# The second MLP matrix by a seven-product block scheme over pairs of token tiles

## The chip, the cores and the metric

One core of a Trainium2 chip runs the whole program. The metric is the device time of one execution in microseconds. Engines: PE (matmul), PEld (its weight loads), DVE (VectorE), ACT (ScalarE), POOL (GpSimd), SP (SyncE, which here only issues transfers).

## The reference

One layer of a hybrid backbone on 128 context and 1024 latent tokens of width 1024: two mixers, then the MLP, which the change is about. All in float32:

```
h = RMSNorm_pre2(x) * (1 + scale2) + shift2
f = square(relu(h @ W1))          # W1: 1024 x 4096
f = f @ W2                        # W2: 4096 x 1024
x = x + gate2 * RMSNorm_post2(f)
```

## The kernel before

There are NT = 1152 tokens in nine tiles of 128. A float32 product is done as three matmuls: each operand is split into a rounded high part (an ACT copy to a reduced form) and a low part (a DVE subtraction), and high·high, high·low and low·high are added in PSUM.

**First matrix.** The 32 hidden blocks of 128 go in pairs p; pairs 0 and 1 plainly (`plain`), pairs 2 to 15 by a block scheme (`strassen`): the operand matrices are cut in two by two blocks, seven products of sums replace eight, and four more steps do the last 384 tokens. A pair is 11 steps of 12 matmuls 128x384. Hooks by step number put the weight sums and splits of the next pair between the steps. `store` (L2087) squares the result and sends it to DRAM (`Fd`).

**Second matrix.** 16 groups g of two hidden blocks each. `g_load` (L2182) reads back the features and two 128x1024 tiles of W2, `g_w` (L2190) and `g_f` (L2197) split them. `mlp2` (L2236) does nine token tiles with two halves of 512 columns each: six matmuls (L2245 to L2247) into one PSUM bank, and a *take*, in which DVE adds the bank to an accumulator in SBUF (L2251), or in group 0 ACT copies it (L2249). The loads and splits for the next group are hooks behind tiles 1, 2, 4 and 6. In the last group `finish_a` and `finish_b` (L2217, L2222) normalize a tile, multiply it with its gate (L2228), add x (L2230, on POOL but for the last tile) and write it out.

Every engine does its row in the order in which the program was written; a tile framework adds semaphores for data, for the reuse of a buffer, and for a pool laid over the room of a closed one. SP issues all transfers of this part, in order: an issue whose data isn't ready holds those behind it.

## Time and profile before

| what | us |
|---|---|
| median of 3 runs | 1738.44 (1736.56 to 1738.83) |
| profiled execution | 1739.05 |
| its span | 1737.3 |
| last pair (p = 15) | 1298.8 to 1321.73 |
| second matrix and output | 1321.73 to 1737.3 |

Busy shares of the span: PE 93%, DVE 64%, ACT 40%, POOL 17%. These are means over stages with different limits, so they don't tell what the second matrix waits for; that is read from its own stretch. 1.75 us of the execution lie outside the span.

### The profile page before, as it was taken

What the parts mean: (1) busy time and instruction counts of PE and PEld (TensorE: products, weight loads), DVE (VectorE), ACT (ScalarE), POOL (GpSimd) and SP (SyncE); (2) the same over time, 40 slices, a digit from 0 to 9 for tenths busy, and PEclk for the clock granted to TensorE, in tenths of its full rate; (3) what the DMA queues carried; (4) which work ended last, traced back from release to release, by engine and by line L of the source; (5) the groups of instructions that cost most, each with busy time, mean ns of one, the idle gap of its engine ahead of it and who ended that gap; (6) DMA issues with size and microseconds to landing.
All of it is one profiled execution on the core that took longest, in us unless ns stands there. A gap on an engine that the chain in (4) does not pass through costs nothing.

```text
span 1737.3 us, 32874 instructions
## 1 busy us (share of the span) xinstructions
...
## 2 busy tenths in 40 slices
...
GB/s 312 189 138 131 208 138 192 160 190 124 148 152 110 162 177 166 198 227 244 199 181 90 123 105 118 121 112 107 94 89 209 77 93 120 115 82 91 140 49 145
DMA packets 317464, 253.09 MB, mean 146 GB/s; under 512 B 102776, under 2 KB 286272, under 8 KB 315264
## 3 DMA queue, kind: packets, MB, share of 16 engines
...
## 4 chain that ended last, share of the span: by engine, by line
PE 70%; DVE 13%; DMA 6%; POOL 5%; issue 2%; ACT 2%; SPq 2%; DVEq 0%; POOLq 0%; ACTq 0%
PE ps_g L2151 7%; PE ps_P L2151 7%; PE ps_g L531 4%; PE ps_G L2151 3%; PE ps_g L532 3%; PE ps_g L533 3%; PE ps_g L1662 3%; POOL ar L1028 2%; POOL ar L1024 2%; PE ps_m L2247 2%; PE ps_g L2247 2%; PE ps_m L2246 2%; PE ps_g L2246 2%; PE ps_m L2245 2%; PE ps_g L2245 2%
## 5 line engine op out<-in xcount | busy, mean ns | idle before, releaser
L531 PE MATMUL ps_g<-hH,wH 128*128 128x384 f32 x552 | 208.5, 378 | 1.8 <-DVE hH L270 1.2
L532 PE MATMUL ps_g<-hL,wH 128*128 128x384 f32 x552 | 191.2, 346 | 5.6 <-DVE hL L484 5.3
L533 PE MATMUL ps_g<-hH,wL 128*128 128x384 f32 x552 | 189.8, 344 | 0.0
L2230 POOL TENSOR_TENSOR rT1H<-rA,rT1H 128x512 f32<-128x512 f32 x2 | 2.9, 1444 | 804.0 <-DVE rA L2228 804.0
L2193 ACT ACTIVATE ws<-w2r 128x1024 fp32r<-128x1024 f32 x32 | 32.4, 1054 | 272.3 <-DVE rA L2251 126.7
L2151 PE MATMUL ps_P<-h2H,ws 128*128 128x384 f32 x448 | 122.7, 334 | 0.0
L531 PEld LDWEIGHTS ps_g<-hH,wH 128*128 128x128 f32 x552 | 107.1, 194 | 17.3 <-issue 8.4
L532 PEld LDWEIGHTS ps_g<-hL,wH 128*128 128x128 f32 x552 | 107.3, 194 | 10.5 <-DVE hL L484 9.3
L533 PEld LDWEIGHTS ps_g<-hH,wL 128*128 128x128 f32 x552 | 107.0, 194 | 0.0
L1028 POOL TENSOR_TENSOR ar<-ar 128x252 f32<-128x252 f32 (+22 forms) x124 | 89.0, 718 | 9.2
L1024 POOL TENSOR_TENSOR ar<-ar 128x252 f32<-128x252 f32 (+22 forms) x124 | 81.1, 654 | 41.6 <-DMA ar<-NAd 32.1
L2151 PEld LDWEIGHTS ps_P<-h2H,ws 128*128 128x128 f32 x448 | 81.7, 188 | 0.0
L2151 PE MATMUL ps_P<-h2L,ws 128*128 128x384 f32 x224 | 74.9, 334 | 0.0
L1539 DVE TENSOR_TENSOR SV<-ps_m,Dt 64x256 f32<-64x256 f32 x136 | 57.0, 421 | 22.7 <-PE ps_m L1534 19.6
L2132 DVE TENSOR_TENSOR ws<-w1r,ws 128x512 fp32r<-128x512 f32 x56 | 37.2, 687 | 53.0 <-ACT ws L2131 53.0
L2251 DVE TENSOR_TENSOR rA<-ps_G,rA 128x512 f32<-128x512 f32 x68 | 46.8, 688 | 36.6 <-PE ps_G L2247 36.6
L1503 PE MATMUL ps_G<-SV,r 128*32 128x64 f32 x1152 | 54.8, 230 | 13.1 <-DVE SV L1539 12.7
L2251 DVE TENSOR_TENSOR rA<-ps_m,rA 128x512 f32<-128x512 f32 x67 | 46.2, 689 | 28.4 <-PE ps_m L2247 28.4
L2251 DVE TENSOR_TENSOR rA<-ps_g,rA 128x512 f32<-128x512 f32 x67 | 46.1, 689 | 27.2 <-PE ps_g L2247 27.0
L1503 PEld LDWEIGHTS ps_G<-SV,r 128*32 128x32 f32 x1152 | 40.7, 114 | 28.1 <-DVE SV L1539 20.4
L1534 PEld LDWEIGHTS ps_m<-SV,IT 128*64 128x64 f32 x1120 | 42.0, 143 | 25.9 <-issue 10.6
L2151 PE MATMUL ps_g<-h2H,ws 128*128 128x384 f32 x224 | 59.3, 335 | 0.0
...
## 6 DMA issues: line engine op xcount, KB each, us to landing
...
```

The costliest lines, as they stand in the source:

```text
L531: T.matmul(ps, wH[:, k, :], hH[b][:, k, :], start=(k == 0), stop=False)
L532: T.matmul(ps, wH[:, k, :], hL[b][:, k, :], start=False, stop=False)
L533: T.matmul(ps, wL[:, k, :], hH[b][:, k, :], start=False, stop=(k == 7))
L1024: E.tensor_tensor(out=t, in0=X[:, :, 0:m, j:j + 1].to_broadcast([128, 2, m, w]), in1=n[:, :, j % 8:j % 8 + 1, j + 1:32].to_broadcast([128, ...
L1028: E.tensor_tensor(out=X[:, :, 0:m, j + 1:32], in0=X[:, :, 0:m, j + 1:32], in1=t, op=ALU.subtract)
L1503: T.matmul(RU[n][r0:r0 + 32, 0, p, :], KRG[n][kq][:, e, p, kc, 0:32], SV[n][s % NSV][:, e, p, :], start=True, stop=True)
L1539: Q.add("V", cv(256), lambda e=e, ks=ks: V.tensor_tensor(out=SV[n][(s + 1) % NSV][ks, e], in0=x["S"][ks], in1=dv[ks], op=ALU.mult), r=[("S ...
L2151: T.matmul(ps[ch], w[:, qw, k], h[q][:, k, :], start=(new and k == n == 0), stop=(k == 3 and n == 2), skip_group_check=True)
L2245: T.matmul(ps, tok(fH, m), wH[:, hs_], start=(m == 0), stop=False)
L2246: T.matmul(ps, tok(fH, m), wL[:, hs_], start=False, stop=False)
L2247: T.matmul(ps, tok(fL, m), wH[:, hs_], start=False, stop=(m == 1))
L2251: V.tensor_tensor(out=acc_(i)[:, hs_], in0=ps, in1=acc_(i)[:, hs_], op=ALU.add)
```

## The change

The second matrix goes by the same kind of scheme. Eight groups have four hidden blocks each (two pairs, e = 0 and 1). Token tile 8 (context) is done plainly, 24 matmuls; tiles (0,3), (1,4), (2,5), (6,7) are pairs u, each done in seven steps s (`STEP2`) of six matmuls 128x512 on sums of feature blocks and of weight blocks, each step with one take. The four x steps add into one PSUM bank, which is taken after each of them.

The sums S1 to S4 of the features are made behind each pair of the first stage (`f_sums`: three POOL adds, one DVE) and stored beside the features; a pair's features now stand in one set of tiles (`ft`) instead of six rotating buffers. The weight sums T1 to T4 are made on POOL (`w_t`); weights and sums are split by `w_s`, high part on ACT, low part on POOL but where `V` is given. Features come back in 128-token tiles (`f_load`) and are split by `f_h` (ACT) and `f_l` (DVE, three pieces); `c_split` does the context tile. In the last pair, STEPZ reorders the steps, and hooks do group 0's loads and splits. The pool `ac` with the accumulators is laid over the closed pool `dp`, in which `ft` and `fS` lie. The finishing is spread over the last group.

```diff
+    Fd = [dr.tile([128, 7, 512], F32, name=f"Fd{p}") for p in range(NP)]
+    Fc = [dr.tile([128, 2, 128], F32, name=f"Fc{p}") for p in range(NP)]
+    pD, pDp = ExitStack(), ExitStack()
...
-    dp = pool_(pD, "dp", 1)
+    wsp = pool_(pD, "wsp", 1)
+    dp = pool_(pDp, "dp", 1)
...
+        put(m // 2, m % 2)
+        if m % 2:
+            f_sums(m // 2)
...
+        if not ft:
+            ft[0], ft[1] = [dp.tile([128, 3, 512], F32, name=f"ft{i}") for i in range(2)]
+            ft["S"] = dp.tile([128, 4, 512], F32, name="fS")
+        if b < 2:
+            f = ft[i][:, b, 0:BLK]
+        else:
+            f, src = ft[i][:, :, BLK:512], src.rearrange("p (a c) -> p a c", a=3)
...
+    def put(p, i, bs=(0, 1)):
+        for b in bs:
+            if (i, b) != (0, 1):
+                SY.dma_start(out=Fd[p][:, i + (b if i else 0)], in_=ft[i][:, b])
+        SY.dma_start(out=Fc[p][:, i], in_=ft[i][:, 2, BLK:512])
+    def f_sums(p):
+        t = ft["S"]
+        (a11, a21), (a12, a22) = [[ft[i][:, b] for b in range(2)] for i in range(2)]
+        G.tensor_tensor(out=t[:, 0], in0=a21, in1=a22, op=ALU.add)
+        V.tensor_tensor(out=t[:, 2], in0=a11, in1=a21, op=ALU.subtract)
+        G.tensor_tensor(out=t[:, 1], in0=t[:, 0], in1=a11, op=ALU.subtract)
+        G.tensor_tensor(out=t[:, 3], in0=a12, in1=t[:, 1], op=ALU.subtract)
+        SY.dma_start(out=Fd[p][:, 3:7], in_=t)
...
+    STEPZ = tuple(STEPS[i] for i in (0, 1, 2, 3, 7, 4, 5, 6, 9, 8, 10))
+        for s_, (wx, hx, ch) in enumerate(STEPZ if p == NP - 1 else STEPS):
...
+            if e in EV:
+                i, b, add = EV[e]
+                store(p, i, b, ps[ch if e != ("S1", "T1") else "z"], {1: t1, 2: u2, 4: u4}.get(add))
+            if e == ("A12", "E2"):
+                put(p, 0, (0,))
             for fn in hooks.get(s_, ()):
                 fn()
+        put(p, 1)
+        f_sums(p)
+    EV = {("A12", "B21"): (0, 0, 1), ("A12", "E2"): (0, 2, 0), ("S1", "T1"): (1, 1, 4), ("A22", "T4"): (1, 0, 2), ("A22", "E2"): (1, 2, 0),
+          ("S4", "B22"): (0, 1, 0)}
...
+    QUAD = ((0, 3), (1, 4), (2, 5), (6, 7))
+    STEP2 = (("A11", "B11", "x"), ("A12", "B21", "y"), ("S2", "T2", "x"), ("S3", "T3", "z"), ("S1", "T1", "x"), ("A22", "T4", "z"),
+             ("S4", "B22", "x"))
+    OPI = {"A11": 0, "A12": 1, "A22": 2, "S1": 3, "S2": 4, "S3": 5, "S4": 6}
...
+    def w_load(g, e, pool):
+        wr2[g, e] = [wp.tile([128, D], F32, tag="raw", name="w2r", bufs=1), pool.tile([128, D], F32, tag="q0", name="w2r2")]
+            r0 = 128 * (2 * (2 * g + e) + i)
+            SY.dma_start(out=wr2[g, e][i], in_=a["w_mlp2"][0, r0:r0 + 128])
...
+        if x in ("T1", "T2"):
+            t = wp.tile([128, 4, 128], F32, tag="mw", name="tt", bufs=2).rearrange("p a b -> p (a b)")
+        else:
+            t = tt2[g, e, {"T4": "T1", "T3": "T2"}[x]]
+        tt2[g, e, x] = t
+        p_, m_ = {"T1": ("B12", "B11"), "T2": ("B22", "T1"), "T4": ("B21", "T2"), "T3": ("B22", "B12")}[x]
+        (E or G).tensor_tensor(out=t, in0=w_raw(g, e, p_), in1=w_raw(g, e, m_), op=ALU.subtract)
+    def w_s(g, e, x, E=None):
+        w = w2[g, e, x] = slot(g, e, x)
+        r = w_raw(g, e, x)
+        S.activation(out=w[:, 0], in_=r, func=AF.Copy)
+        (E or G).tensor_tensor(out=w[:, 1], in0=r, in1=w[:, 0].bitcast(F32), op=ALU.subtract)
...
+    def f_l(u, e, c, E=None):
+        H, L = fo(u, e)
+        (E or V).tensor_tensor(out=L[:, c], in0=fr[e][:, c], in1=H[:, c].bitcast(F32), op=ALU.subtract)
+    PC = (slice(0, 2), slice(2, 4), slice(4, 7))
...
+    def c_split(e):
+        H, L = fo(0, e)
+        S.activation(out=H[:, 7:9], in_=cr[:, e], func=AF.Copy)
+        V.tensor_tensor(out=L[:, 7:9], in0=cr[:, e], in1=H[:, 7:9].bitcast(F32), op=ALU.subtract)
...
+    def take(g, i, h, ps, first=False):
+        if g == 0 and first:
+            S.activation(out=acc_(i, h), in_=ps, func=AF.Copy)
+        else:
+            V.tensor_tensor(out=acc_(i, h), in0=ps, in1=acc_(i, h), op=ALU.add)
...
+        for u, (i, j) in enumerate(QUAD):
+            ps = {}
+            for s_, (fx, wx, ch) in enumerate(STEP2):
+                new = ch not in ps
+                if new:
+                    ps[ch] = bank(CH[ch])
+                for e in range(2):
+                    f, w = fo(u, e), w2[g, e, wx]
+                    for n, (qf, qw) in enumerate(TERMS):
+                        T.matmul(ps[ch], f[qf][:, OPI[fx]], w[:, qw], start=(new and e == n == 0), stop=(e == 1 and n == 2),
+                                 skip_group_check=True)
+                take(g, *((i, 0), (i, 0), (j, 0), (j, 1), (j, 1), (j, 0), (i, 1))[s_], ps[ch], s_ in (0, 2, 3, 6))
+                run(hooks, (u, s_))
...
+        for u in range(4):
+            gn, un = (g, u + 1) if u < 3 else (g + 1, 0)
+            if gn == NG2:
+                break
+            gl, ul = (g, u + 2) if u < 2 else (g + 1, u - 2)
+            for e in range(2):
+                add(u, 3 * e, lambda un=un, e=e: f_h(un, e))
+                for n in range(3):
+                    add(u, 3 * e + n, lambda un=un, e=e, n=n: f_l(un, e, PC[n], G if last and e else None))
+                if gl < NG2:
+                    add(u, 3 * e + 2, lambda gl=gl, ul=ul, e=e: f_load(gl, ul, e))
+        if last:
+            return hk
+        n = g + 1
+        add(3, 6, lambda: c_split(0), lambda: c_split(1))
+        add(0, 6, lambda: c_load(n))
+        sp = lambda e, x, E=None: lambda: w_s(n, e, x, E)
+        tt = lambda e, x: lambda: w_t(n, e, x)
+        add("c", 0, sp(0, "B11"))
+        add(0, 0, sp(0, "B12"))
...
+        add(0, 5, tt(0, "T1"))
+        add(1, 0, sp(0, "T1"), tt(0, "T2"))
+        add(1, 2, sp(0, "T2"), tt(0, "T4"))
+        add(1, 4, sp(0, "T4"), tt(0, "T3"))
+        add(1, 5, lambda: w_load(n, 1, mp["ac"]))
...
+        add(3, 1, sp(1, "T1", V), tt(1, "T2"))
+        add(3, 2, sp(1, "T2", V), tt(1, "T4"))
+        add(3, 3, sp(1, "T4"), tt(1, "T3"))
...
+            sp = lambda e, x, E=None: lambda: w_s(0, e, x, E)
+            tt = lambda e, x: lambda: w_t(0, e, x)
+            lf = [lambda: f_load(0, 0, 0), lambda: f_load(0, 0, 1), lambda: c_load(0)]
+            hooks = {0: lf + [lambda: w_load(0, 0, dp)],
+                     2: [rooms, tt(0, "T1"), sp(0, "B22", V)],
+                     3: [sp(0, "T1"), tt(0, "T2"), sp(0, "B11", V)],
+                     4: [sp(0, "T2"), tt(0, "T4"), sp(0, "B21", V)],
+                     5: [lambda: c_split(0), lambda: f_h(0, 0), tt(0, "T3")] + [lambda c=c: f_l(0, 0, c) for c in PC],
+                     6: [lambda: c_split(1), lambda: f_h(0, 1)] + [lambda c=c: f_l(0, 1, c) for c in PC] +
+                        [lambda: f_load(0, 1, 0), lambda: f_load(0, 1, 1), sp(0, "T4")],
+                     7: [rooms2, sp(0, "B12", V), lambda: w_load(0, 1, dp), sp(0, "T3")],
+                     8: [rooms3, sp(1, "B11", V), tt(1, "T1"), sp(1, "B21", V)],
+                     9: [sp(1, "B12", V), sp(1, "T1"), tt(1, "T2"), sp(1, "B22", V)],
+                     10: [sp(1, "T2"), tt(1, "T4"), tt(1, "T3")]}
         strassen(p, hooks)
+    w_s(0, 1, "T4", V)
+    w_s(0, 1, "T3", V)
+    pDp.close()
+    mp["ac"] = pool_(pD, "ac", 1)
+    DD[1] = act_slots(0)
+    w_load(1, 0, mp["ac"])
...
+            for h in range(2):
+                hooks.setdefault(("c", h), []).extend([lambda h=h: g2.make(h), lambda h=h: g2.load(h + 2)])
+                hooks[0, h] = [lambda h=h: g2.make(h + 2)] + hooks[0, h]
...
+    nc = bacc.Bacc("TRN2", target_bir_lowering=False, num_devices=1, dynamic_dma_scratch_size=8192)
```

SP, from the sums of pair 14 to the loads of group 1 (Fd_10105 and on are the features of pairs 0 and on, so Fd_10119 is pair 14). Before:

```order
L2095 DMA Fd_10119<-f 128x384 x6
L2095 DMA Fd_10120<-f 128x384 x2
L2184 DMA rT2H<-Fd_10105 128x2304
L2187 DMA w2r<-in_w_mlp_dram 128x1024
L2187 DMA w2r_13402<-in_w_mlp_dram 128x1024
L2095 DMA Fd_10120<-f 128x384 x4
```

After, first the loads of group 0:

```order
L2115 DMA Fc_10135<-ft_10161 128x128
L2124 DMA Fd_10119<-fS 128x2048
L2277 DMA fr_10562<-Fd_10105 128x7x128
L2277 DMA fr_10563<-Fd_10106 128x7x128
L2289 DMA cr<-Fc_10121 128x256
L2289 DMA cr<-Fc_10122 128x256
L2240 DMA w2r<-in_w_mlp_dram 128x1024
L2240 DMA w2r_13327<-in_w_mlp_dram 128x1024
L2114 DMA Fd_10120<-ft_10160 128x512
L2115 DMA Fc_10136<-ft_10160 128x128
```

and, further on, the loads for e = 1 of group 0, the stores of pair 15 and the first load for group 1:

```order
L2240 DMA w2r<-in_w_mlp_dram 128x1024
L2240 DMA w2r_13477<-in_w_mlp_dram 128x1024
L2114 DMA Fd_10120<-ft_10161 128x512 x2
L2115 DMA Fc_10136<-ft_10161 128x128
L2124 DMA Fd_10120<-fS 128x2048
L2240 DMA w2r<-in_w_mlp_dram 128x1024
L2240 DMA w2r_13563<-in_w_mlp_dram 128x1024
```

The store of pair 14's sums (L2124) now stands ahead of all loads of group 0, and that of pair 15 ahead of the load for group 1.

ACT, in the last pair. Before (u are results kept for later sums, f the stores, ws the weight copies of group 0):

```order
L2154 ACTIVATE t_13310<-ps_g 128x384
L2090 ACTIVATE f<-ps_P 128x384
L2091 ACTIVATE f<-f 128x384
L2154 ACTIVATE u_13311<-ps_g 128x384
L2154 ACTIVATE u_13312<-ps_g 128x384
L2193 ACTIVATE ws<-w2r 128x1024
L2193 ACTIVATE ws<-w2r_13402 128x1024
L2203 ACTIVATE rT2L<-rT2H 128x576 x4
L2090 ACTIVATE f<-ps_P 128x384
L2091 ACTIVATE f<-f 128x384
```

After, in the same place (L2188 u, L2105 and L2106 the stores, L2261 the weight copies, tt the sums T, w2r_13327 the second raw W2 tile):

```order
L2188 ACTIVATE t_13305<-ps_g 128x384
L2261 ACTIVATE sH_13358<-w2r_13327 128x512
L2105 ACTIVATE ft_10160<-ps_P 128x3x128
L2106 ACTIVATE ft_10160<-ft_10160 128x3x128
L2261 ACTIVATE sH_13358<-tt 128x512
L2261 ACTIVATE s_13360<-w2r 128x512
L2261 ACTIVATE sL_13359<-tt 128x512
L2261 ACTIVATE s_13361<-w2r_13327 128x512
L2188 ACTIVATE u_13306<-ps_g 128x384
L2293 ACTIVATE fT2H<-cr 128x256
L2280 ACTIVATE fT2H<-fr_10562 128x896
```

and where group 0 begins (acc_13579 is the context tile's accumulator):

```order
L2105 ACTIVATE ft_10160<-ps_g 128x384
L2106 ACTIVATE ft_10160<-ft_10160 128x384
L2261 ACTIVATE sH_13496<-tt 128x512 x2
L2261 ACTIVATE sL_13497<-tt 128x512
L2306 ACTIVATE acc_13579<-ps_s 128x512
L2261 ACTIVATE sL_13497<-w2r 128x512
L2306 ACTIVATE acc_13579<-ps_P 128x512
L2306 ACTIVATE acc_13604<-ps_g 128x512
L2280 ACTIVATE fT1H<-fr_10562 128x896
```

Six weight copies and two pairs of feature copies moved in among the copies and stores that PE waits for, and the takes of group 0 stand behind and between copies of POOL's sums.

DVE in a steady group. Before, from one split to the next (L2194 weights, L2204 features, L2251 takes):

```order
L2194 TENSOR_TENSOR ws<-w2r,ws 128x1024
L2251 TENSOR_TENSOR rA_13555<-ps_m,rA_13555 128x512
L2251 TENSOR_TENSOR rA_13555<-ps_G,rA_13555 128x512
L2194 TENSOR_TENSOR ws<-w2r_14836,ws 128x1024
L2251 TENSOR_TENSOR rA_13555<-ps_s,rA_13555 128x512
L2251 TENSOR_TENSOR rA_13555<-ps_P,rA_13555 128x512
L2251 TENSOR_TENSOR rA_13592<-ps_g,rA_13592 128x512
L2251 TENSOR_TENSOR rA_13592<-ps_m,rA_13592 128x512
L2204 TENSOR_TENSOR rY_14965<-rT3L,rY_14964 128x576 x4
```

After, the last pair of tiles of a group, steps 0 to 4 (L2308 takes, L2284 feature pieces, L2262 weight splits):

```order
L2308 TENSOR_TENSOR acc_13836<-ps_g,acc_13836 128x512
L2284 TENSOR_TENSOR fT2L<-fr_10562,fT2H 128x256
L2308 TENSOR_TENSOR acc_13836<-ps_m,acc_13836 128x512
L2284 TENSOR_TENSOR fT2L<-fr_10562,fT2H 128x256
L2262 TENSOR_TENSOR s_13360<-tt,s_13360 128x512
L2308 TENSOR_TENSOR acc_13859<-ps_g,acc_13859 128x512
L2284 TENSOR_TENSOR fT2L<-fr_10562,fT2H 128x384
L2262 TENSOR_TENSOR s_13362<-tt,s_13362 128x512
L2308 TENSOR_TENSOR acc_13859<-ps_G,acc_13859 128x512
L2284 TENSOR_TENSOR fT3L<-fr_10563,fT3H 128x256
L2308 TENSOR_TENSOR acc_13859<-ps_g,acc_13859 128x512
L2284 TENSOR_TENSOR fT3L<-fr_10563,fT3H 128x256
```

and its end with the next group's first takes (L2294 the context tile's split):

```order
L2308 TENSOR_TENSOR acc_13859<-ps_G,acc_13859 128x512
L2284 TENSOR_TENSOR fT3L<-fr_10563,fT3H 128x384
L2308 TENSOR_TENSOR acc_13836<-ps_g,acc_13836 128x512
L2294 TENSOR_TENSOR fT2L<-cr,fT2H 128x256
L2294 TENSOR_TENSOR fT3L<-cr,fT3H 128x256
L2308 TENSOR_TENSOR acc_13579<-ps_s,acc_13579 128x512
L2308 TENSOR_TENSOR acc_13579<-ps_P,acc_13579 128x512
```

Between two takes there is now a feature piece nearly everywhere, a weight split twice, and the context splits stand behind the last take of the group.

## Rows read from the trace of the kernel before

**Rows 1.** Table of stretches: stretch, length, busy (count) by engine, PEclk, DMA share, GB/s.

```profile
1209.00:1321.00 112.00, 112.00 (x647) 112.00 (x646) 51.57 (x85) 43.79 (x82) 0.00 (x0) 1.00 0.32 107
1321.00:1697.00 376.00, 376.00 (x1629) 305.55 (x1628) 248.76 (x353) 75.57 (x111) 0.00 (x0) 1.00 0.30 105
```

**Rows 2.** The same view for one group of the second matrix.

```profile
1371.30:1396.10 24.80, 24.80 (x108) 20.00 (x107) 16.84 (x24) 3.79 (x6) 0.00 (x0) 1.00 0.26 91
```

**Rows 3.** Chain that ended last: start, duration, work; last pair and first group.

```profile
1319.65 2.08 PE ps_g L2151 x12
1321.73 0.23 PE ps_g L2245
```

**Rows 4.** Timeline of the end: start, duration, engine, line, tiles, [idle <-releaser].

```profile
1720.80 0.40 PE L2247 MATMUL ps_P<-ws,rY 128*128 128x512 f32 x1
...
1727.16 1.06 ACT L2219 ACTIVATE jk<-rA 128x1024 f32<-128x1024 f32 x1 [2.09 <-DVE rA L2251]
...
1728.34 0.29 ACT L2220 ACTIVATE ss<-ss,eps 128x1 f32<-128x1 f32 x1
...
1733.53 0.69 DVE L2230 TENSOR_TENSOR rT3H<-rA,rT3H 128x512 f32<-128x512 f32 x1
```

**Rows 5.** Timeline of two DVE takes in a row.

```profile
1363.99 0.68 DVE L2251 TENSOR_TENSOR rA<-ps_m,rA 128x512 f32<-128x512 f32 x1
...
1364.60 0.68 DVE L2251 TENSOR_TENSOR rA<-ps_G,rA 128x512 f32<-128x512 f32 x1
```

**Rows 6.** Lines by form, 1321 to 1697: count, busy, mean ns, idle before.

```profile
L2194 DVE TENSOR_TENSOR ws<-w2r,ws 128x1024 fp32r<-128x1024 f32 x30 | 36.5, 1218 | 10.2 <-ACT ws L2193 10.2
...
L2204 DVE TENSOR_TENSOR rY<-rT3L,rY 128x576 fp32r<-128x576 f32 x32 | 22.1, 751 | 1.3 <-ACT rY L2203 1.3
```

**Rows 7.** The same view for POOL, from 700 us on.

```profile
L1873 POOL TENSOR_TENSOR r<-r,bv 128x512 f32<-128x512 f32 x6 | 7.7, 1281 | 78.1 <-ACT r L1869 32.4 <-DMA bv<-Bd 26.9 <-ACT SV L268 18.8
L2230 POOL TENSOR_TENSOR rT2L<-rA,rT2L 128x512 f32<-128x512 f32 x4 | 6.3, 1582 | 1.3 <-issue 0.7 <-DVE rA L2228 0.6
```

**Rows 8.** Timeline of DVE products beside POOL adds.

```profile
1702.80 1.41 DVE L2228 SCALAR_TENSOR_TENSOR rA<-rA,ss,rX 128x512 f32<-128x512 f32 x2
...
1704.75 0.69 DVE L2251 TENSOR_TENSOR rA<-ps_g,rA 128x512 f32<-128x512 f32 x1
...
1705.34 1.29 POOL L2230 TENSOR_TENSOR rT1H<-rA,rT1H 128x512 f32<-128x512 f32 x1
...
1705.55 1.64 DVE L2228 SCALAR_TENSOR_TENSOR rA<-rA,ss,rX 128x512 f32<-128x512 f32 x1
```

**Rows 9.** Timeline of ACT where the last pair begins.

```profile
1298.86 0.49 ACT L2090 ACTIVATE f<-ps_g 128x384 f32<-128x384 f32 x1 [1.03 <-PE ps_g L2151]
1299.39 0.52 ACT L2091 ACTIVATE f<-f 128x384 f32<-128x384 f32 x1
1299.82 0.61 ACT L2131 ACTIVATE ws<-w1r 128x512 fp32r<-128x512 f32 x1
```

**Rows 10.** Timeline of the loads for the first group.

```profile
1309.25 0.32 SPq L2184 DMA_DIRECT2D rT2H<-Fd  x1
...
1309.62 0.90 SPq L2187 DMA_DIRECT2D w2r<-in_w_mlp_dram  x2
...
1316.91 1.06 ACT L2193 ACTIVATE ws<-w2r 128x1024 fp32r<-128x1024 f32 x1 [0.20 <-DMA w2r<-in_w_mlp_dram]
```

**Rows 11.** DMA rate in 40 slices of 1308 to 1318 us.

```profile
GB/s 0 0 0 0 221 387 178 0 147 258 74 111 295 295 479 442 442 332 516 406 406 406 340 361 426 410 475 393 393 442 393 475 305 395 252 31 0 0 0 0
```

**Rows 12.** Table of stretches around one dip of PEclk.

```profile
932.30:935.70 3.40, 2.36 (x11) 1.30 (x10) 3.29 (x9) 2.52 (x6) 0.00 (x0) 1.00 0.42 161
935.70:939.10 3.40, 3.40 (x13) 3.04 (x12) 2.38 (x6) 2.91 (x7) 0.00 (x0) 0.50 0.00 0
```

**Rows 13.** Gate products: ns min/median/max, first and last start.

```profile
L1740 DVE TENSOR_TENSOR rX<-rX,mw x4: 683/683/683, 1497.4 to 1572.0; 128x512 f32<-128x512 f32 x4
```

More of the change, by code (lines that the diff above doesn't have):

```diff
@@ L2147, in strassen @@
             if new:
-                ps[ch] = bank(CH[ch], BLK)
+                ps[ch] = bank("s" if ch == "v" and p == NP - 1 else CH[ch], BLK)
             for k in range(4):
@@ new lines, in hymba_kernel, with act_slots, slot @@
+    TX = ("T1", "T4", "T2", "T3")
+    R, DD, SB = [None] * 3, [None] * 2, []
+    hw = {}
+    def act_slots(n):
+        if n not in hw:
+            hw[n] = [act.tile([128, 3, 2, 512], F32R, tag=f"h{q}{n}", name=f"s{q}{n}") for q in "HL"]
+        return [hw[n][i][:, j] for i in range(2) for j in range(3)]
+    def slot(g, e, x):
+        if x == "B12":
+            return SB[e]
+        if x in ("B11", "B21"):
+            return R[-g % 3][2 * e + (x == "B21")]
+        if x != "B22" and e:
+            return R[(1 - g) % 3][TX.index(x)]
+        return DD[g % 2][e if x == "B22" else 2 + TX.index(x)]
@@ new lines, in hymba_kernel, with fo, f_load @@
+    fr = [wsp.tile([128, 7, 128], F32, name=f"fr{e}") for e in range(2)]
+    cr = wsp.tile([128, 2, 2, 128], F32, name="cr")
+    FT2, fop = {}, {}
+    def fo(u, e):
+        k = u % 2, e
+        if k not in FT2:
+            x = {(0, 0): "T2", (0, 1): "T3", (1, 0): "T1", (1, 1): "T4"}[k]
+            FT2[k] = [tb.tile([128, 12, 128], F32R, tag=f"o{x}{q}", name=f"f{x}{q}") for q in "HL"]
+        return FT2[k]
+    def f_load(g, u, e):
+        SY.dma_start(out=fr[e], in_=Fd[2 * g + e][:, :, 128 * u:128 * u + 128])
@@ L2217, in finish_a, with acc_ @@
+    TERMS = ((0, 0), (0, 1), (1, 0))
+    acc_t, x1_t, fin_ss, gt2, xs = {}, {}, {}, {}, []
+    def acc_(i, h):
+        if i not in acc_t:
+            acc_t[i] = mp["ac"].tile([128, D], F32, name=f"acc{i}")
+        return acc_t[i][:, 512 * h:512 * h + 512]
+    def take(g, i, h, ps, first=False):
[3 more added lines that the diff above has]
+            V.tensor_tensor(out=acc_(i, h), in0=ps, in1=acc_(i, h), op=ALU.add)
     def finish_a(i):
-        ss = fin_ss[i] = dp.tile([128, 1], F32, tag="ss", name="ss", bufs=2)
@@ L2229, in finish_b @@
                                    op1=ALU.mult)
[L2230 to L2231 removed]
+            (V if i == FIN[-1] else G).tensor_tensor(out=xt[:, hs_], in0=t[:, hs_], in1=xt[:, hs_], op=ALU.add)
+            if end:
                 SY.dma_start(out=dst[:, hs_], in_=xt[:, hs_])
[L2233 removed]
+        if not end:
             SY.dma_start(out=dst, in_=xt)
[L2236 to L2259 removed]
```

208 lines of the change are left out of this document (96 added, 112 removed).

## Prediction, made before the changed kernel ran

> **What bounds the kernel now.** I read the table of stretches first: in the last 112 us of the first matrix and in nearly all of the second PE is busy all the time at full clock (376.00 of 376.00 us), DVE two thirds of it (248.76), POOL not at all [rows 1]. A window of one group shows 108 matmuls in 24.80 us with DVE at 16.84 [rows 2]; the groups come every 24.86 us, so 230 ns a matmul. So what bounds the second matrix is the count of its matmuls. The chain of waits then gives the place where it starts: a step of the first matrix (12 matmuls) is 2.08 us, and the last ends at 1321.73 [rows 3]. The timeline of the end shows the last matmul ending at 1721.20, the last add at 1734.22 and the span at 1737.3: a tail of 16.1 us [rows 4], in which DVE works off what it had got behind.
>
> **What the change removes.** A group of two old ones does 24 + 4·42 = 192 matmuls of the old shape for 216, so 8 groups have 1536 for 1728: 192 · 0.230 = 44.1 us. The ideal group is 44.15 us. DVE takes 30 banks for 36, 0.69 each and, back to back, 0.61 apart [rows 5]; but the 128x1024 splits of w2 (1.22 on DVE [rows 6]) become sixteen blocks and sums to split, and the feature splits come in many small pieces. The last group of before took some 2.0 us more than 24.86 (1321.73 + 15·24.86 = 1694.6 to 1721.2); the new tail spreads nine finishes over its last group and leaves, behind the last matmul, a take 0.7, square and root 1.6, two tiles' products and adds some 4 and an output of 3.1 (1734.22 to 1737.3): 9.5 for 16.1 [rows 4].
>
> **What it adds, steady groups.** POOL gets 22 operations of 128x512 a group (8 sums, 14 of the 16 splits). Its price alone is 1.28 us, beside DVE 1.58 [rows 7], so 28 to 35 us of a 44 us group: it fits. The timeline of the tail shows the other price: a DVE product with two SBUF inputs took 0.70 alone (two in 1.41) and 1.64 when begun 0.21 us behind a POOL add of 1.29, while a take with one PSUM input stayed at 0.69 beside POOL [rows 8]. So takes don't suffer, and the feature splits do (24 pieces and two for the context tile a group, 256 or 384 wide: some 0.34 and 0.48 by width from the 128x576 split's 0.75 [rows 6]; no row has these widths).
>
> The Trainium skill, in "SBUF — State Buffer", section "Who interferes with whom", says that a DVE instruction with two SBUF inputs and a GpSimd instruction that reads SBUF exclude each other, the second being blocked fully. The trace agrees (1.64 for 0.70). By it alone, with every POOL operation meeting a DVE one, the group would go by POOL; that is a rival below.
>
> Three places are left where PE waits in a steady group. (a) The two context splits stand on DVE behind the take of (3,6), so the next group's third matmul waits for take, ACT copy and split: 0.65 to 1.7, I take 1.0. (b) At (3,1) and (3,2) DVE does two weight splits itself (0.69 each by the adds of that size) between takes and feature pieces; all x products go through one bank, so the step after next can't start before the take: 0.75 to 1.5, I take 1.1. (c) An ACT copy that waits for POOL stands ahead of the feature copy: 0.5; scatter 0.6. Sum 3.2, bounds 1.0 (the copies early, no locks) and 5.5. Six groups at 47.3: 283.8.
>
> **The hand-over (pair 15 to group 0).** Times from the start of the last pair, whose 11 steps ideally take 22.9 us.
> 1. The feature sums of pair 14 need its last store, which ends 1.1 us in (1298.86 to 1299.91; the pair starts at 1298.8) [rows 9]; then three chained POOL adds at 1.28 to 1.69: to 5.0 to 6.3, with hand-offs 6.5. SP is in order: the store of these sums (1 MB) stands ahead of the two feature loads, two context loads and two w2 loads, where before nothing of the kind did.
> 2. SP takes 0.32 to 0.45 an issue. Before, 2.2 MB issued at 1309.25 were there by 1316.91, 7.7 us [rows 10]. Here 3.2 MB lie ahead of the end of the second w2 tile: 11 us, so 17.5 (at some 450 GB/s, as in the better slices of that stretch [rows 11], 15).
> 3. ACT, in order, has the copy of a block of that second tile at step 2, due 6.3. Behind it stand a store, four copies that partly wait for POOL sums and splits, and then the u copy of step 5. Copies of 0.61 [rows 9] and POOL at 1.3 to 1.6 put that at 24. Step 7 of PE needs the bank and was due at 14.6: 9.4 us of waiting. Then the feature copies and their DVE pieces go before the u4 copy and the stores: 4 more. The pair ends at 36.3 instead of 22.9.
> 4. The second hidden-block pair's w2 has the same two raw buffers, so it waits for the last POOL and DVE reads of the first, at 33, and lands at 38. POOL's remaining sums and splits run to 47.7, and only then come the feature sums of pair 15, to 52; their store lands at 56.
> 5. The accumulators lie over the room of these sums, so ACT's first take of group 0 waits for that store. The takes of group 0 are ACT's, in order, and step (0,2) needs the bank of (0,0): it starts at 60.6 for an ideal 31.15. That is 29.5 late. Bounds: 17 when no POOL operation is locked, the loads come at 15 and PE isn't held in the pair; 35 when each POOL operation takes 1.69.
> Then 1.7 for the clock: one stretch of 3.4 us at 0.50 stands in the trace [rows 12], the lower of two levels (1.2 GHz), behind idle stretches of PE; and 4 for the rest of group 0, whose ACT takes stand behind copies that wait for POOL. Group 0: 44.15 + 35.2 = 79.4. What hides the sums of pairs 0 to 14 is PE's own work: they take POOL 5 us of a 22.9 us pair, with 0.7 us left before the feature tiles are written again at step 2; if that is missed ACT waits, not PE, whose next use of the bank is 2 steps off. Cost nothing, up to 1 a pair.
>
> **The last group.** DVE has 30 takes at 0.61 = 18.3, pieces 3.5, eight gate products at 0.69 = 5.5 [rows 13], seven finishes at 1.6 (0.15 and 1.41) = 11.2, and POOL's adds lock seven times 0.9 = 6: 44.5 for PE's 44.15, and the first gate product stands in DVE's row ahead of the takes and waits for rows that are loaded when the group begins (4 us). I take 8.4 for both, 4 to 11: 52.5.
>
> **The sum.** 1321.7 + 79.4 + 283.8 + 52.5 + 9.5 = 1746.9 for a span of 1737.3; with the 1.75 around it 1748.7 for 1739.05 of the profiled execution. That stands 0.6 above the median of 1738.44, so 1748. Instructions ahead of the first stage stand as they did. POOL's own transfers have a smaller scratch (8192); no row shows its price, and I take 0, -3 to 3.
>
> **Rivals.**
> A, the other side: the hand-over's POOL chain is short. It decides at ACT's first take. If the first weight sums finish unhindered and the last feature sums are stored by 42 us, that take costs 13 to 17 and not 29.5, and group 0 follows without the 4. For it: DVE had 51.57 of 112 us of work in the last pairs [rows 1], so locks may be rare. Against it: 17 POOL operations in one in-order row, each with an ACT copy before it. 1748 - 14 - 4 = 1730, to 1720 if the steady groups lose 1.5.
> B: locks make POOL the bound. 22 operations at 1.69 are 37, the waits for ACT copies between sum and split 5, and idle at the loads 6 to 8: 48 to 50 a group. Six at 50 add 16: 1764. For it the 1.64; against it, DVE is in a take or idle most of the time.
> C: the matmuls saved aren't got, since with x products in one bank each step waits for a take. 44 more, less what the stalls share: 1775.
>
> **How the numbers follow.** The sum 0.50 (its own range 1738 to 1759), A 0.32 (1717 to 1738), B 0.13 (1758 to 1772), C 0.05. A measurement of this kernel can tell 0.2%, 3.5 us, from no change: 1735 to 1742. Faster: A but for its upper edge, 0.30, and what the sum could miss by, 0.02. Same: 0.13. Slower: 0.55. Range: both ends that leave a tenth outside, 1718 to 1768.
>
> **What would show it.** The sum is right if the profile after shows PE idle twice in the last pair and once at the start of group 0, some 30 us together, released by ACT takes and w2; group distances of 46 to 48; DVE near full in the last group; the last matmul less than 11 us before the end. Step 1 is wrong if the w2 loads are issued before 5 us into the pair. It is wrong as a whole if group 0 starts its second accumulation less than 20 us late (A), if POOL is busy over 80% of a steady group (B), or if matmuls are not 230 ns apart where PE waits for nothing (C).

## The result

The changed kernel takes 1798.96 us (median of 4 runs, 1793.63 to 1803.65); the kernel before takes 1738.63 in the same runs. The ratio is 1.0346 with a 95% interval of 1.0311 to 1.0381. The forecast was 1748 with a range to 1768: the sign was right and the size far off. The profiled execution has a span of 1794.5, against a worked sum of 1746.9. The first matmuls of pair 2 and of the groups, and the end of pair 14's last matmul (1298.8 before, 1296.5 after), cut both into the same stretches:

| stretch | worked | measured |
|---|---|---|
| ahead of pair 2 (new in it are only the sums of pairs 0 and 1) | 990.4 | 985.1 |
| pairs 2 to 14 | 308.4 | 311.5 |
| pair 15 and group 0 | 102.3 | 110.7 |
| groups 1 to 6 | 283.8 | 310.1 |
| group 7 and the end | 62.0 | 77.2 |

The first stretch varied between 982.9 and 994.6 over the profiled executions told of below, which don't differ in it, so there only what follows it is compared.

The table of stretches of the changed kernel: the last 112 us of the first matrix, one steady group, and three parts of group 7 (columns as in [rows 1]).

```profile
1209.00:1321.00 112.00, 102.12 (x588) 101.58 (x586) 58.78 (x83) 39.57 (x77) 23.90 (x17) 0.97 0.44 146
1511.18:1562.57 51.39, 46.29 (x194) 35.36 (x193) 40.72 (x59) 17.02 (x27) 29.93 (x23) 1.00 0.37 118
1717.31:1731.50 14.19, 8.89 (x37) 6.60 (x36) 7.26 (x11) 2.92 (x6) 1.01 (x1) 0.94 0.80 259
1731.50:1746.70 15.20, 11.08 (x25) 8.10 (x26) 7.94 (x15) 0.47 (x1) 4.30 (x5) 0.61 0.40 144
1746.70:1782.70 36.00, 32.27 (x132) 23.94 (x130) 27.29 (x45) 11.93 (x22) 21.23 (x19) 1.00 0.49 165
```

PE, full in [rows 1, 2], now has gaps in every one of them. In the steady group no engine is full: DVE 40.72 and POOL 29.93 of 51.39. So it is not one engine's amount of work that sets the group; something is late in turn. The chain of waits through one of its gaps, ahead of step 6 of tile pair 2, from here on (2,6), shows what (start, duration, work; "issue" is time that no wait explains):

```profile
1540.86 5.62 DMA w2r<-in_w_mlp_dram
1546.47 0.02 issue
1546.49 0.02 ACT s L2261
...
1547.03 0.94 ACT fT4H L2280
...
1548.68 0.69 DVE acc L2308
1549.37 0.04 issue
1549.41 0.73 PE ps_g L2364 x2
```

A W2 tile lands at 1546.47. ACT's copy of it (L2261) stands ahead of the feature copy (L2280); behind that copy, on DVE, a feature piece, and behind the piece the take (L2308) for which PE waits. PE needs neither the tile nor the feature piece yet. The same place in the timeline (columns as in [rows 4]):

```profile
1546.49 0.63 ACT L2261 ACTIVATE s<-w2r 128x512 fp32r<-128x512 f32 x1 [5.24 <-DMA w2r<-in_w_mlp_dram]
...
1547.99 0.76 DVE L2284 TENSOR_TENSOR fT4L<-fr,fT4H 128x256 fp32r<-128x256 f32 x1 [2.79 <-ACT fT4H L2280]
1548.68 0.68 DVE L2308 TENSOR_TENSOR acc<-ps_g,acc 128x512 f32<-128x512 f32 x1
...
1549.41 0.73 PE L2364 MATMUL ps_g<-sH,fT2H 128*128 128x512 f32 x2 [2.13 <-DVE acc L2308]
```

and where the next group begins:

```profile
1562.35 1.63 DVE L2284 TENSOR_TENSOR fT3L<-fr,fT3H 128x384 fp32r<-128x384 f32 x1
...
1563.90 0.68 DVE L2308 TENSOR_TENSOR acc<-ps_g,acc 128x512 f32<-128x512 f32 x1
1564.51 0.41 DVE L2294 TENSOR_TENSOR fT2L<-cr,fT2H 128x256 fp32r<-128x256 f32 x1
...
1564.97 0.50 PE L2351 MATMUL ps_s<-sL,fT2L 128*128 128x512 f32 x1 [1.67 <-DVE fT2L L2294]
```

Here a feature piece of 128x384 took 1.63 beside a POOL split, locked like the 1.64 of [rows 8]; it took 0.55 alone. It delays the take, and the context split behind it ends last.

The hand-over in the timeline: DVE's sum of pair 14, the store of the sums, the loads, ACT's copy of the second W2 tile, the u copy, PE's step; then ACT's first takes of group 0 and the copy between them.

```profile
1302.84 0.68 DVE L2121 TENSOR_TENSOR fS<-ft 128x512 f32<-128x512 f32 x1
...
1303.58 0.32 SPq L2124 DMA_DIRECT2D Fd<-fS  x1
...
1308.51 0.91 SPq L2240 DMA_DIRECT2D w2r<-in_w_mlp_dram  x2
...
1315.11 0.63 ACT L2261 ACTIVATE sH<-w2r 128x512 fp32r<-128x512 f32 x1 [12.85 <-DMA w2r<-in_w_mlp_dram]
...
1321.29 0.47 ACT L2188 ACTIVATE u<-ps_g 128x384 f32<-128x384 f32 x1
...
1321.81 0.69 PE L2183 MATMUL ps_g<-oT1H,ws 128*128 128x384 f32 x1 [10.69 <-ACT u L2188]
...
1353.39 0.60 ACT L2306 ACTIVATE acc<-ps_s 128x512 f32<-128x512 f32 x1 [4.05 <-POOL fS L2123]
...
1353.81 1.33 SPq L2240 DMA_DIRECT2D w2r<-in_w_mlp_dram  x2
1359.58 0.63 ACT L2261 ACTIVATE sL<-w2r 128x512 fp32r<-128x512 f32 x1 [5.60 <-DMA w2r<-in_w_mlp_dram]
...
1361.24 1.22 PE L2364 MATMUL ps_g<-sL,fT2H 128*128 128x512 f32 x2 [13.14 <-ACT acc L2306]
```

Group 7: DVE's gate products wait twice for their rows, and takes behind them hold PE.

```profile
1727.54 0.69 DVE L1740 TENSOR_TENSOR fzH<-fzH,mw 128x512 f32<-128x512 f32 x1 [4.50 <-DMA mw<-in_b_mod_dram]
...
1731.54 1.22 PE L2364 MATMUL ps_g<-sL,fT2H 128*128 128x512 f32 x2 [3.67 <-DVE acc L2308]
...
1736.33 0.69 DVE L1740 TENSOR_TENSOR fzH<-fzH,mw 128x512 f32<-128x512 f32 x1 [4.84 <-DMA mw<-in_b_mod_dram]
...
1741.00 1.22 PE L2364 MATMUL ps_g<-sH,fT2H 128*128 128x512 f32 x2 [4.08 <-DVE acc L2308]
...
1782.70 0.39 PE L2364 MATMUL ps_g<-sH,fT4L 128*128 128x512 f32 x1
```

### The profile page after: what moved, and what is told of

The parts are those of the page before. It is cut to its first block, busy times and chain, and to the rows that moved or that the text cites. A ratio compares the mean times of both kernels' runs of the same rounds, so it can differ in the third digit from the quotient of the medians.

```text
span 1794.5 us, 33111 instructions
## 1 busy us (share of the span) xinstructions
PE 1608.5 (90%) x13035; PEld 1341.2 (75%) x13035; DVE 1204.9 (67%) x1933; ACT 758.8 (42%) x1401; POOL 614.3 (34%) x650
## 3 DMA queue, kind: packets, MB, share of 16 engines
q8 instruction: 102, 1.67, 0.4%
## 4 chain that ended last, share of the span: by engine, by line
PE 50%; DVE 15%; POOL 14%; DMA 10%; issue 5%; ACT 5%; SPq 1%; another core or an unknown queue 0%; DVEq 0%; POOLq 0%; ACTq 0%
PE ps_g L2183 6%; PE ps_P L2183 6%; POOL ar L1028 4%; POOL ar L1024 4%; PE ps_g L2364 3%; PE ps_g L531 3%; PE ps_G L2183 3%; DMA w2r<-in_w_mlp_dram 3%; PE ps_g L532 3%; PE ps_g L533 3%; PE ps_g L1662 3%; POOL tt L2255 2%; DVE acc L2308 2%; PE ps_m L1534 2%; PE ps_G L1503 2%
## 5 line engine op out<-in xcount | busy, mean ns | idle before, releaser
L2120 POOL TENSOR_TENSOR fS<-ft,ft 128x512 f32<-128x512 f32 x16 | 21.5, 1343 | 337.4 <-ACT ft L2106 337.4
L2183 PE MATMUL ps_P<-h2H,ws 128*128 128x384 f32 x432 | 118.4, 334 | 0.0
L2308 DVE TENSOR_TENSOR acc<-ps_g,acc 128x512 f32<-128x512 f32 x116 | 78.9, 684 | 24.7 <-PE ps_g L2364 23.2
L2161 DVE TENSOR_TENSOR ws<-w1r,ws 128x512 fp32r<-128x512 f32 x56 | 47.7, 873 | 52.3 <-ACT ws L2160 52.3
L1534 PE MATMUL ps_m<-SV,IT 128*64 128x64 f32 x1120 | 51.0, 232 | 8.3 <-DVE SV L1539 5.7
L2160 ACT ACTIVATE ws<-w1r 128x512 fp32r<-128x512 f32 x56 | 34.8, 625 | 52.7 <-DMA w1r<-in_w_mlp_dram 42.3
L268 ACT ACTIVATE SV<-ps_G 32x256 f32<-32x256 f32 x95 | 35.7, 376 | 45.0 <-PE ps_G L1519 33.2
```

What stands on the lines that cost most here:

```text
L1534: T.matmul(x["S"][64 * e:64 * e + 64, p, :], it_()[:, e, p, :], sv_()[:, e, p, :], start=True, stop=True)
L2183: T.matmul(ps[ch], w[:, qw, k], h[q][:, k, :], start=(new and k == n == 0), stop=(k == 3 and n == 2), skip_group_check=True)
L2308: V.tensor_tensor(out=acc_(i, h), in0=ps, in1=acc_(i, h), op=ALU.add)
```

## The experiments

Theory M: each engine does its row in order, and what costs is a thing that comes late standing ahead of one that PE needs. Theory L: POOL's work and its lock against DVE bound the group, in any order. All kernels, by stretch (from the first matmuls in their traces):

| kernel | pairs 2 to 15 | group 0 | groups 1 to 6, mean | group 7 and end | time | before, same runs |
|---|---|---|---|---|---|---|
| changed | 349.8 | 72.4 | 51.68 | 77.2 | 1798.96 | 1738.63 |
| e1_csplit | 350.2 | 72.4 | 49.48 | 76.5 | 1785.61 | 1736.86 |
| e2_b11 | 349.6 | 70.2 | 51.04 | 76.3 | 1789.57 | 1736.86 |
| e8_narrow | 349.9 | 76.4 | 47.03 | 73.9 | 1772.91 | 1736.86 |
| e4_fsput | 343.1 | 76.4 | 51.26 | 77.6 | 1795.31 | 1736.86 |
| e9_early | 349.9 | 70.8 | 47.88 | 76.9 | 1770.44 | 1739.36 |
| e5_b11g0 | 351.3 | 67.7 | 51.16 | 76.7 | 1794.61 | 1739.36 |
| e6_gate | 350.0 | 74.2 | 51.67 | 68.2 | 1793.00 | 1739.36 |
| e7_dvehand | 345.2 | 69.9 | 51.72 | 77.2 | 1789.85 | 1739.36 |
| e10_all | 335.1 | 62.5 | 47.67 | 67.3 | 1739.94 | 1737.85 |
| e11_next | 334.7 | 51.9 | 46.49 | 70.1 | 1726.85 | 1741.90 |
| e12_narrow2 | 334.5 | 52.7 | 44.74 | 70.7 | 1717.42 | 1739.44 |
| e13_dvepieces | 334.2 | 52.1 | 46.35 | 77.2 | 1732.06 | 1739.44 |

PE's idle time and its clock are to be told apart in these stretches. First the rows of group 0 in the changed kernel, e4_fsput and e8_narrow, then those of groups 1 to 6 together in the changed kernel, e1_csplit, e2_b11 and e8_narrow (columns as in [rows 1]):

```profile
1334.86:1407.23 72.37, 48.63 (x194) 36.37 (x193) 40.29 (x48) 31.78 (x54) 42.09 (x31) 0.91 0.34 111
```

```profile
1333.83:1410.21 76.38, 54.07 (x193) 40.59 (x192) 39.78 (x48) 31.76 (x54) 41.78 (x31) 0.82 0.32 104
```

```profile
1335.17:1411.58 76.41, 53.91 (x193) 40.44 (x192) 39.82 (x48) 31.79 (x54) 41.83 (x31) 0.84 0.32 104
```

```profile
1407.23:1717.31 310.08, 283.30 (x1152) 216.64 (x1152) 242.18 (x347) 102.22 (x157) 178.71 (x133) 0.98 0.37 117
```

```profile
1413.77:1710.67 296.90, 278.93 (x1153) 212.11 (x1152) 251.28 (x348) 103.52 (x159) 181.66 (x134) 1.00 0.39 123
```

```profile
1409.99:1716.22 306.23, 284.24 (x1152) 220.13 (x1152) 237.42 (x347) 103.67 (x157) 179.77 (x133) 0.96 0.38 119
```

```profile
1411.58:1693.77 282.19, 275.07 (x1152) 214.12 (x1153) 211.27 (x347) 104.55 (x158) 86.79 (x133) 1.00 0.41 129
```

The same matmuls keep PE busy longer where its mean granted clock (PEclk) is lower. In groups 1 to 6 of the changed kernel four stretches of 3.4 us ran at 0.50, the lower of two levels (1.2 GHz). Each began 0.5 to 1.8 us behind the end of a wait of 1.7 to 2.1 us; this one did so 1.0 us behind the wait of 1.67 that ended at 1564.97:

```profile
1566.00:1569.40 3.40, 3.40 (x9) 2.65 (x8) 0.60 (x1) 0.34 (x1) 0.85 (x1) 0.50 0.39 114
```

**The context splits earlier.**

```diff
-        add(3, 6, lambda: c_split(0), lambda: c_split(1))
+        add(1, 6, lambda: c_split(0))
+        add(2, 6, lambda: c_split(1))
```

> Edit: the two splits of the context tile's features stand behind steps (1,6) and (2,6) of the group before, not behind (3,6). Theory M (engines held in order by late neighbours): the wait between the second and the third matmul of a group, 2.07 us in the changed kernel, falls to 0.23, so each of groups 1 to 7 is 1.8 us shorter (51.7 to 49.9) and the whole about 13 us below 1799: 1786. Theory L (POOL and the locks bound the group): the wait turns up elsewhere, groups stay within 0.6 us of 51.7 and the time within 4 us of 1799.

Groups fell by 2.2 us: M, and somewhat more than the gap itself. PE's idle time fell by 1.5 a group, and its busy time by 0.7 at the higher clock. The wait ahead of (2,6) shrank too, to 0.74 at most, and one of 1.06 appeared ahead of (2,2).

**The ACT copies of the second block pair behind the feature copy.** B11, B12 and B21 of e = 1 go to (2,3), (2,4), (2,5).

> Edit: ACT's first copies of the second pair of W2 blocks stand one to two steps later, behind the feature copy of (2,3). Theory M: PE's wait of 2.3 us ahead of step (2,6), which comes from this copy waiting for its load, goes or falls below 0.4; groups 1 to 6 go from 51.7 to 49.4, the whole about 13 us below 1799: 1786. Theory L: groups within 0.6 us of 51.7, time within 4 us of 1799.

The gap of 2.1 ahead of (2,6) went, but a new one of 2.31 stands at (3,4); the groups gained 0.6 only. PE's idle time fell by 0.8 a group, and its busy time rose by 0.2 at a clock of 0.96. The copies, later by one to two steps, push POOL's sums and with them DVE's weight split at (3,1) ahead of a take:

```profile
1555.09 1.21 DVE L2262 TENSOR_TENSOR s<-tt,s 128x512 fp32r<-128x512 f32 x1 [1.84 <-ACT s L2261]
...
1556.22 0.68 DVE L2308 TENSOR_TENSOR acc<-ps_g,acc 128x512 f32<-128x512 f32 x1
...
1556.95 1.22 PE L2364 MATMUL ps_g<-sH,fT1H 128*128 128x512 f32 x2 [2.31 <-DVE acc L2308]
```

So my expectation of M failed here. By this chain the load itself is too late: moving its user only moves the wait.

**POOL's splits narrow.** This kernel leaves out most of the low parts of the weights.

```diff
+        n = 32 if g > 1 and E is None else 512
-        (E or G).tensor_tensor(out=w[:, 1], in0=r, ...
+        (E or G).tensor_tensor(out=w[:, 1, 0:n], in0=r[:, 0:n], ...
```

> Edit: from group 2 on, POOL's weight splits are 32 columns wide instead of 512 (14 of its 22 operations in a group), so the low parts of the weights are not computed anew; all else stands. Theory M: POOL is not what PE waits for; only the locked stretches of feature splits shrink: groups 2 to 7 from 51.5 to 49.5 to 50.8. Theory L: with two thirds of POOL's work and locks gone groups fall to 46 or less, some 33 us in the whole.

47.0: neither. POOL's splits cost 4.6 us a group in this order (3.3 of PE's idle time, 1.4 of its busy time at the lower clock), far more than M alone had allowed. The wait ahead of (2,6) is 0.20 in one group and gone in the others, and the third matmul of a group waits 0.65 for 1.67. In group 3 ACT's copy still waits 5.29 for the W2 load, but in all six groups it now comes 1.0 to 1.5 us before the end of step (2,4), where it came up to 0.6 behind it. A locked piece and a late result would both explain the gain. The next run, and the same edit on a mended order, part them only in part.

**The weight chain spread anew**, with the edit of the context splits:

```diff
-        add("c", 0, sp(0, "B11"))                                (and the rest of the list)
+        add("c", 1, tt(0, "T1"), sp(0, "B21"))
+        add(0, 1, sp(0, "T1"), tt(0, "T2"))
+        add(0, 3, sp(0, "T2"), tt(0, "T4"))
+        add(0, 5, sp(0, "T4"), tt(0, "T3"))
+        add(1, 1, sp(0, "T3"), lambda: w_load(n, 1, mp["ac"]))
+        add(3, 0, sp(1, "T2"))
+        add(3, 1, sp(1, "T1"), tt(1, "T4"))
...
```

> Edit: the context splits as in the kernel with them at (1,6) and (2,6), and the whole weight chain of a group spread anew: the first block pair's sums and splits from (c,1) on, its successor's W2 load at (1,1), the second pair's from (1,6), the four splits that must wait for (3,1) in (3,0) to (3,3), all on POOL. POOL's count of operations and their width are unchanged (24 for 22). Theory M (what costs is that results come late in an in-order row): groups 1 to 6 fall from 49.4 with the context edit alone to 46.5 to 47.5. Theory L (what costs is the locks and POOL's amount of work, as its narrow splits' 47.0 suggests): no better than 49.

47.88, with POOL busy 33.30 us of a group (it took over DVE's two splits) and all widths unchanged. So 1.6 us a group below the first edit came with more work on POOL, against L. How much of it is the order and how much the two splits that DVE no longer does, this run doesn't show.

**The hand-over, three edits apart.** The store of pair 14's sums behind the loads:

```diff
-            hooks = {0: lf + [lambda: w_load(0, 0, dp)],
+            hooks = {0: lf + [lambda: w_load(0, 0, dp), lambda: fs_put(NP - 2)],
```

> Edit: the store of the feature sums of pair 14 is issued behind the six loads of group 0. Theory M: the loads go out 6.5 us sooner, ACT's copy of the second W2 tile with them, and PE's wait in the last pair (11.0 us) falls to 3 to 5; the last pair ends 6 to 8 us sooner and the whole is about 7 us shorter: 1792. Rival (the wait is for the bytes of the loads themselves, 3.2 MB either way): the wait falls by 2 us at most. A second rival: what is gained is lost again in group 0, which waits for POOL's chain and the next W2 load; then group 0 begins sooner but its third step doesn't.

The last pair ended 6.7 us sooner, as M had it, and the third step of group 0 came 6.9 sooner (57.8 for 64.7 from the pair's start), against the second rival. Group 0 took 4.0 longer all the same. Its idle time fell by 1.4, but PE was busy 5.4 longer, at a mean clock of 0.82 for 0.91. The kernel with the narrow splits, which changes nothing in group 0, took 76.4 there too, at 0.84. So what group 0 gave back was the clock, and up to 4 us of one group 0 against another is no effect of an edit.

Group 1's first ACT copies behind (0,3) of group 0:

> Edit: in group 0 alone, the ACT copies of group 1's first two weight blocks stand behind step (0,3) and not among the first takes. Theory: the 13.5 us wait before the third step of group 0 is 7.6 of POOL's sums and 6 of the W2 load that such a copy waits for; the wait falls to 7 to 8 and group 0 from 72.4 to 67, less what the later copies hold up (up to 3). If the take itself waited for the store of the sums, nothing changes.

The wait fell from 13.5 to 7.3 (from matmul to matmul) and group 0 to 67.7, as expected: 6 us of it were the load for the next group. PE's idle time in group 0 fell by 6.6, so this is more than the clock.

The weight sums and splits of the last pair by DVE (`w_t(0, e, x, V)`, `w_s(0, e, x, V)`):

> Edit: in the last pair all weight sums and splits for group 0 are made by DVE instead of POOL. Theory (POOL's length and the locks hold the hand-over): 14 operations at 0.69 and without locks instead of 1.3 to 1.8; ACT's copies come sooner, the wait of 13.5 us in group 0, which ends 5.6 us after POOL's last sum, falls by 6 to 10, and so does the whole: about 1790. Rival (the two W2 loads set it): under 3 us.

Pairs 2 to 15 and group 0 fell by 7.1 together, and the wait to 8.3. POOL's work did hold it, by its length or by the locks: this run takes away both.

**The gate products later in group 7.**

> Edit: in the last group the four gate products stand at (0,3), (0,4), (1,2), (1,3) instead of between the first takes, and the finishing of tiles 8, 3 and 0 later with them. Theory: PE's waits of 4.1 and 4.6 us, which end with takes behind products that wait for gate rows, go, and with them the 14 us at half clock behind (about 7 us); the later finishing costs up to 3 at the end. Group 7 and what follows fall from 77.2 to 59 to 64, the whole to about 1783. Rival (DVE is full in this group, and the order doesn't matter): 74 or more.

9 us less, and 3.4 us at half clock are left of 13.6. But waits of 2.4 and 2.8 us came up behind the finishing: half to two thirds of the expected gain, the rival in part.

**Together, with a new hand-over.**

> Edit: the edits that paid, together (context splits earlier, weight chain spread anew, gate products later in the last group), and a new hand-over: the W2 loads of group 0 ahead of its feature loads, both ahead of the store of pair 14's sums; the first block pair's sums by DVE, its last raw read two steps sooner, so that the second W2 load goes out at step 5 and not 7; the load for group 1 ahead of the store of pair 15's sums; group 1's first copies behind (0,2) of group 0. Theory M: steady groups 47.5, group 7 and end 67, and the hand-over, whose pair and group 0 took 110.7 us for an ideal 67, loses 10 to 15 instead of 44: sum 1297 + 67 + 12 + 6*47.5 + 67 = 1728 for the span, 1725 to 1735 for the time, 0.3 to 0.8% below the kernel before. Rival (the hand-over is held by the amount of DVE and ACT work in the last pair, some 25 us of DVE for 22.9 of PE): hand-over loses 25 or more, time 1740 to 1750.

The ratio to the kernel before is 1.0001 (0.9982 to 1.0021): 59 us won back, not the gain that was expected. The pair has no wait over 0.5 us left, but group 0 lost 18: ACT's takes stand behind copies that wait for POOL (4.62, 2.83 and 2.96), and PE's mean clock there was 0.91.

**What group 0 and the feature pieces cost.**

```diff
+        elif g == 0 and first:
+            V.tensor_copy(out=acc_(i, h), in_=ps)
+            add("c", 0, lambda: f_l(0, 1, PC[2]), lambda: f_load(g, 1, 1))
...
+            if h and not end:
+                S.activation(out=t[:, hs_], in_=t[:, hs_], func=AF.Copy, scale=ss)
+                G.tensor_tensor(out=t[:, hs_], in0=t[:, hs_], in1=gt, op=ALU.mult)
```

> Edit on top of all the edits together: (A) the last two weight splits of group 0 and, for the last pair alone, the feature sums on DVE, behind the first take; (B) in group 0 the first takes of the last three tile pairs by DVE, not ACT, and group 1's POOL-fed copies later; (C) the last two feature pieces of a group one to two steps later, the third behind the next group's first take; (D) in the last group half of each finished tile scaled by ACT and multiplied by POOL. Theory M (late neighbours in in-order rows): group 0 from 62.5 to 50 to 54, steady groups from 47.6 to 46 to 46.5, last group from 55.4 to 50: 20 to 25 us less than 1740, so 1715 to 1720, 1.0 to 1.3% below the kernel before. Theory L (DVE and POOL hold each other up whatever the order): steady groups stay within 0.5 of 47.6 and the time above 1730.

1726.85, ratio 0.9907 (0.9885 to 0.9928): faster than both kernels. Group 0 fell to 51.9 and the steady groups to 46.49, as M had it. The time missed M's 1715 to 1720, because of the last group: its matmuls took as long as before the edit and its end 3 us longer. So (D), together with the later load that (C) brings there, paid nothing.

**POOL's splits narrow on this order.**

> Edit: the kernel of the run before (46.5 us a steady group) with POOL's weight splits 32 columns wide from group 2 on, so that their low parts aren't computed anew. Theory M: with the orders mended what is left (2.3 us over 44.15) is the takes and copies on the x bank and a share of locks; groups 1 to 6 from 46.5 to 45.5 to 46. Theory L: locks are all that is left: 44.5 or less. Against the 51.5 to 47.0 of the same edit in the changed kernel: a fall of under 1.5 us here means that most of those 4.5 us were lateness which the order made costly, not the lock as such.

The same edit that gave 4.6 us in the changed order gives 1.75 here, between the two expectations, and a little over the 1.5 under which most of the 4.6 was to count as lateness. The rows of a group, first of the kernel above, then of this one:

```profile
1472.15:1518.93 46.78, 45.78 (x194) 35.49 (x192) 40.20 (x57) 17.25 (x26) 33.49 (x25) 1.00 0.41 130
```

```profile
1464.01:1508.78 44.77, 44.77 (x194) 35.94 (x192) 33.86 (x56) 17.13 (x26) 15.08 (x24) 1.00 0.44 136
```

DVE's busy time falls by 6.3 us with POOL's 18.4: that is what the locks cost DVE. PE gained 1.75, from the locks or from what POOL now has ready sooner; no run parts these two.

**Feature pieces of group 7 back on DVE.**

> Edit: on the kernel of the run before last, the last group's feature pieces of the second block pair go back from POOL to DVE. Theory: PE's waits of 1.25, 0.69, 2.18 and 1.28 us ahead of their matmuls in the last group go, since POOL stands in front of them with the finishing; DVE takes on 4 us of work and some of it comes back as late takes: last group from 55.3 to 51 to 53, time 1723 to 1726, 1.0 to 1.2% below the kernel before. Rival (DVE is full in that group): no change within 1 us.

Worse by 7 us in the last group, against both expectations. The load for these pieces comes late in that group, and on DVE the piece now stands ahead of a take:

```profile
1671.33 0.95 ACT L2285 ACTIVATE fT4H<-fr 128x896 fp32r<-128x896 f32 x1 [8.42 <-DMA fr<-Fd]
1672.32 0.43 DVE L2289 TENSOR_TENSOR fT4L<-fr,fT4H 128x256 fp32r<-128x256 f32 x1 [5.38 <-ACT fT4H L2285]
...
1673.99 0.68 DVE L2315 TENSOR_TENSOR acc<-ps_g,acc 128x512 f32<-128x512 f32 x1
...
1674.73 1.22 PE L2375 MATMUL ps_g<-sH,fT2H 128*128 128x512 f32 x2 [5.72 <-DVE acc L2315]
```

In the kernel above ACT's copy waited as long for the same load (8.22), and PE lost 0.85, at the step that reads the copy. This is M at its plainest. In this run a second late piece (4.37) cost PE 3.73 in the same way.

## Why the prediction was wrong

**The step that failed** is "Three places are left where PE waits in a steady group", with its sum of 3.2. The groups lost 7.5 each (51.68 against 44.15), which over six is 26 us more than the sum had; the sum had them faster than two old groups (49.9), and they were slower. Of its three terms, in the group shown and from matmul to matmul, (a) was 1.84 for 1.0: the piece ahead of the take was locked, which the 1.64 of [rows 8] would have told. (b) was 1.6 for 1.1, two waits of 0.65 and 0.96. (c) named the wrong releaser: the ACT copy in front of the feature copy waits for the W2 *load*, not for POOL, and that made 2.3 for 0.5 (1.7 to 2.3 over the six groups). The three make 5.7. Of the rest, 0.6 in the sum, about 1.1 a group is the clock, an estimate from the four stretches of 3.4 us at 0.50 with PE busy throughout; the sum had the clock in the hand-over alone. I had looked for the load's place in SP's row in the hand-over and not in the groups, though it is the same pair of raw buffers. By experiment, 51.68 goes to 49.48 (context splits), to 47.88 (weight chain), to 46.49 (feature pieces later) and to 44.74 (POOL's splits narrow): 5.2 of the 7.5 went with edits of the order, one of which also took two splits off DVE, 1.75 with POOL's splits, and 0.6 is left. These shares hold for this sequence of edits; made first, the narrow splits gave 4.6.

One reading under the sum was off as well. Fifteen groups of the kernel before take 374.73 us:

```profile
1321.57:1696.30 374.73, 374.73 (x1621) 304.41 (x1621) 247.69 (x352) 75.37 (x110) 0.00 (x0) 1.00 0.30 105
```

That is 24.98 a group and not 24.86, and 231 ns a matmul. The ideal group is 44.4 and not 44.15, and the 2.0 us by which the last group was said to be longer aren't there. Over eight groups this is 2 us.

**The last group** lost 21.6 us to the end of its last matmul (65.8 for 44.15) against 8.4. DVE's work came to 42.9 us for the 44.5 of the sum; it was the waiting that was wrong. That the gate rows come late was in the sum once, with 4; the rows were waited for twice (4.50 and 4.84), because the second pair of loads is issued only after the first products, at 1728.98. What the five loads of x ahead of it add was not tried. Then PE ran at a mean granted clock of 0.61 for 15 us, which the sum did not have for this group at all. The end took 11.4 for 9.5.

**The hand-over** was right in its steps and nearly in size: PE's wait in the pair 10.69 for 9.4, pair end at 38.3 for 36.3, the second W2 load issued at 35.3 for 33, POOL's last sum done at 56.9 for 52, step (0,2) at 64.7 for 60.6 (all from the pair's start, 1296.5). The clock took some 4.3 for 1.7, an estimate from 5.3 us of PE's work in the pair and 3.4 in group 0 at 0.50, and five waits behind step (0,2) took 6.7 for 4. Two releasers were wrong. The store of pair 14's sums went out behind DVE's sum (L2121, done at 1303.53), when POOL's last had been done at 1302.37. And ACT's first take did not wait for the store of the sums to land, only for POOL's last sum; the 5.6 us behind it were the W2 copy between the takes.

**The rivals.** A did not come. B, POOL as the bound at 50 a group, came close in its number for another reason: POOL was busy 29.93 of 51.39, 58% for the 80% that was to show B. C was wrong: where PE waits for nothing the matmuls are 0.23 apart, and with the orders mended more than half of the 44 us are there: e11_next's groups 1 to 6 take 46.49 for two old ones' 49.9.

**Pairs 2 to 14** lost 3 us, within the bound of 1 a pair; nothing was tried on them.
